# Layer-0 norm weights by a product with ones, squares and fold out of PSUM, new load costs in the planner

## The chip, the cores and the metric

The kernel runs on one core of a Trainium2 chip. The metric is the device time of one execution in microseconds; the median of several executions is compared. The engines are TensorE (PE, with its weight loads shown apart as PEld), VectorE (DVE), ScalarE (ACT), GpSimd (POOL) and SyncE (SP), which issues all the DMA transfers here.

## The reference

A two-layer encoder trunk takes one step for 512 prompt tokens and 64 sample tokens (576 rows of 1024 channels). Each layer norms x, makes one wide projection, runs three mixers (differential attention, sparse attention with a learned index, retention), gates and merges them, and adds an output projection to x. Keys, values and states are outputs too. Cut to its frame:

```python
for l in range(DEPTH):                       # 2 layers; 1024 cached keys for the sample rows
    z = rmsnorm(x, norm_g[l]) @ w_in[l]      # 1024 x 8132, split into the operands of A, B, C and the gates
    oa = diff_attention(...)                 # A: 4 heads, two softmax maps each, T5 bias
    ob = dsa_attention(...)                  # B: lightning index, top-k keys, 8 heads
    oc = rmsnorm(retention(...), c_gn_g[l])  # C: 4 heads with decay, rotary, running state
    br = stack([oa * silu(ag), ob * silu(bg), oc * silu(cg)])
    proj = einsum('btnw,nwd->btnd', br, w_branch[l])
    x = x + sum(sigmoid(mg) * proj) @ w_out[l]

def rmsnorm(x, g):
    return x * rsqrt(mean(x * x, -1) + EPS) * g
```

## The kernel before

**Tiles.** The 576 rows stand in five tiles of rows, four of 128 and one of 64 (the sample). Every large product is made of three: operands are split into a rounded part (hi) and the rest (lo), and PE adds hi x hi, hi x lo and lo x hi in one PSUM accumulation. `wload` (line 535) fetches a weight block of 512 rows x 256 columns by DMA into `wraw`, casts it on ACT to `whi` (line 549) and subtracts on DVE, or on POOL where the step is marked with `*`, to `wlo` (line 550). `wload_idx` (line 555) does the same for the index weights with casts in line 566. `proj_tok` (line 659) and `proj_ch` (line 682) are the loops of matmuls over such blocks.

**Stages.** Per layer `x_norm(t)` (line 590) squares a tile of x on ACT with a running sum (line 601, in layer 0 alone), takes the power -0.5 of the mean on POOL (line 507), scales the tile by that and by the norm weights on DVE (line 611), and transposes it on PE by products with the identity into a PSUM tile named `s` (line 616), from where ACT casts it to `xh` (line 618) and DVE subtracts it to `xl`. The norm weights `gx` are two tiles `P` of 128 x 512, which a DMA with a partition step of 0 fills (line 587). Line 804 is the index projection, the first large product of a layer, line 1018 the transposes of queries and keys of mixer A, line 1070 its logits. At the end of the layer `out_proj(u)` (line 1369) runs for either half of 512 columns: for each row tile it loads the residual into `xr` (a tile named `sg`), makes 24 matmuls into a PSUM tile `pj` (line 1402; for the sample tile 16 matmuls whose lower half ACT copies to `up`, a tile `P`, in line 1396, and which DVE adds back), scales and adds on DVE (line 1405) and, in layer 0, squares the result on ACT into a PSUM tile `s` for the running sum of the next layer's norm (line 1411; only the sum is used).

**Buffers.** Tiles of one name take turns in a fixed number of buffers: two `sg`, four `P`, four `r`, two `wraw`, three `whi`, two `wlo`; in PSUM three `pj`, two `s`, three `t`. A new tile waits until the last use of the one that had its buffer.

**Order.** The program is traced once in the order of `STEPS` (lines 90 to 128), one string per layer. A step is a name, a number and a `*` or not, and up to four biases. Then `Order.plan()` (line 279) puts all instructions into an order by a list scheduler: each has a cost by `_cost`, waits cost `LAG` and `SLOT`, and whenever an engine is free the ready instruction goes first whose traced position plus bias is least. The biases belong to PE, to the other engines, to SP, and to a spread over the step. `pin()` fixes the order of each engine. So an engine works strictly in this order, and an instruction that is not ready holds up all behind it. DMAs are in SP's order; the scheduler has a cost for each, from its bytes and the length of its contiguous runs.

## Time and profile before

| | |
|---|---|
| time of three runs | median 1425.64 us, from 1422.21 to 1428.57 |
| time of the profiled execution | 1423.9 us |
| span of the profiled execution | 1422.1 us |
| mean granted PE clock | 0.993 |
| PE busy | 1370.1 us, 96% of the span |
| DVE busy | 1030.6 us, 72% |
| ACT busy | 718.5 us, 51% |
| POOL busy | 383.0 us, 27% |
| DMA | 129.60 MB, 32% of 16 DMA engines |

The span runs from the first to the last instruction of the profiled execution; its time has 1.8 us more round it. Shares of an engine are shares of the span, and PE's own busy time counts its matmuls, whether at full clock or at half. An engine's idle time is put down to what released it: the last semaphore before the instruction that ended the wait. A granted clock of 1.00 is the full one, 2.4 GHz, and 0.50 the lower level, 1.2 GHz.

### The profile page before, as it was taken

What the parts mean: (1) busy time and instruction counts of PE and PEld (TensorE: products, weight loads), DVE (VectorE), ACT (ScalarE), POOL (GpSimd) and SP (SyncE); (2) the same over time, 40 slices, a digit from 0 to 9 for tenths busy, and PEclk for the clock granted to TensorE, in tenths of its full rate; (3) what the DMA queues carried; (4) which work ended last, traced back from release to release, by engine and by line L of the source; (5) the groups of instructions that cost most, each with busy time, mean ns of one, the idle gap of its engine ahead of it and who ended that gap; (6) DMA issues with size and microseconds to landing.
All of it is one profiled execution on the core that took longest, in us unless ns stands there. A gap on an engine that the chain in (4) does not pass through costs nothing.

```text
span 1422.1 us, 26631 instructions
## 1 busy us (share of the span) xinstructions
PE 1370.1 (96%) x9974; PEld 1296.9 (91%) x9974; DVE 1030.6 (72%) x2517; ACT 718.5 (51%) x1733; POOL 383.0 (27%) x356
## 2 busy tenths in 40 slices
PE   6999999999999999999989999999999999999998
PEld 5999999999989999998789999999989999899976
DVE  6689799997766787553378567999987777765442
ACT  5543455566656666432253344655546667565320
POOL 1633353344332300100130473412421333010000
PEclk9999999999999999999989999999999999999999
DMA  8533332343422312234432221434322312222343
GB/s 201 145 94 87 100 101 85 79 108 94 102 66 63 90 51 79 74 104 130 132 116 66 68 78 49 128 92 110 99 75 67 80 46 73 60 67 60 90 137 100
DMA packets 179994, 129.60 MB, mean 91 GB/s; under 512 B 65452, under 2 KB 168920, under 8 KB 179864
## 3 DMA queue, kind: packets, MB, share of 16 engines
q1 hardware_dynamic: 179864, 127.90, 32.2%
q8 instruction: 78, 1.28, 0.4%
q14 instruction: 52, 0.43, 0.1%
HBM read 114.84 MB, written 13.03 MB: 90 GB/s over the span
## 4 chain that ended last, share of the span: by engine, by line
PE 55%; DVE 9%; DMA 4%; ACT 4%; issue 2%; POOL 1%; DVEq 0%; ACTq 0%; POOLq 0%; SPq 0%
PE pj L690 28%; PE pj L678 7%; PE pj L1402 5%; DMA wraw<-in_w_in_dram 2%; DMA wraw<-in_w_out_dram 2%; PE s L1253 1%; DVE wlo L550 1%; PE t L1266 1%; DVE u L885 1%; POOL wlo L550 1%; DVE m L884 1%; ACT whi L549 1%; PE s L1070 1%; DVE s L520 1%; PE t L1085 1%
## 5 line engine op out<-in xcount | busy, mean ns | idle before, releaser
L550 POOL TENSOR_TENSOR wlo<-wraw,whi 128x1024 fp32r<-128x1024 f32 x62 | 151.2, 2452 | 311.4 <-PE pj L690 183.7
L549 ACT CAST whi<-wraw 128x1024 fp32r<-128x1024 f32 x148 | 155.2, 1049 | 138.6 <-DMA wraw<-in_w_in_dram 79.5
L690 PE MATMUL pj<-xh,whi 128*128 128x288 f32 x1216 | 206.0, 300 | 4.7 <-ACT whi L549 2.2
L690 PE MATMUL pj<-xh,wlo 128*128 128x288 f32 x1216 | 202.3, 298 | 0.2 <-DVE wlo L550 0.2
L690 PE MATMUL pj<-xl,whi 128*128 128x288 f32 x1216 | 202.1, 297 | 0.0
L690 PEld LDWEIGHTS pj<-xh,whi 128*128 128x128 f32 x1216 | 174.0, 188 | 8.7 <-ACT whi L549 3.3
L690 PEld LDWEIGHTS pj<-xl,whi 128*128 128x128 f32 x1216 | 174.9, 188 | 1.1
L690 PEld LDWEIGHTS pj<-xh,wlo 128*128 128x128 f32 x1216 | 174.2, 188 | 1.9 <-DVE wlo L550 0.6
L550 DVE TENSOR_TENSOR wlo<-wraw,whi 128x1024 fp32r<-128x1024 f32 x86 | 110.0, 1291 | 60.0 <-PE pj L690 49.1
L690 PE MATMUL pj<-u,whi 128*128 128x288 f32 x768 | 124.8, 297 | 0.1
L678 PE MATMUL pj<-whi,xh 128*128 128x256 f32 x768 | 116.1, 283 | 2.6 <-DVE ssn L701 1.7
L507 POOL TENSOR_TENSOR ssn<-ssn,mh 128x4 f32<-128x4 f32 (+1 forms) x70 | 67.8, 972 | 179.5 <-DVE ssn L506 160.1
L678 PE MATMUL pj<-wlo,xh 128*128 128x256 f32 x768 | 115.8, 283 | 0.0
L884 DVE MAX8 m<-u 128x8 f32<-128x1088 f32 (+2 forms) x128 | 113.5, 888 | 1.5
L678 PE MATMUL pj<-whi,xl 128*128 128x256 f32 x768 | 113.1, 281 | 0.0
L885 DVE MATCH_REPLACE8 u<-m,u 128x1088 f32<-128x1088 f32 (+2 forms) x128 | 112.0, 875 | 0.1
L690 PEld LDWEIGHTS pj<-u,whi 128*128 128x128 f32 x768 | 109.4, 189 | 1.7 <-DVE sg L1348 0.6
L678 PEld LDWEIGHTS pj<-whi,xh 128*128 128x128 f32 x768 | 100.3, 188 | 5.2 <-DVE ssn L701 2.7
L678 PEld LDWEIGHTS pj<-wlo,xh 128*128 128x128 f32 x768 | 100.0, 188 | 1.5 <-issue 0.3
L678 PEld LDWEIGHTS pj<-whi,xl 128*128 128x128 f32 x768 | 98.6, 188 | 0.8 <-issue 0.5
L728 POOL TENSOR_TENSOR u<-r,u 128x512 fp32r<-128x512 f32 x24 | 31.9, 1339 | 172.5 <-ACT u L727 172.4
L1339 ACT ACTIVATE sg<-pj 128x288 f32<-128x288 f32 x96 | 38.9, 410 | 61.4 <-PE pj L690 60.9
(299 smaller groups left out, 2694.9 us busy)
## 6 DMA issues: line engine op xcount, KB each, us to landing
wraw<-in_w_in_dram SPq DMA_DIRECT2D x116, 512.0 KB, 3.8
wraw<-in_w_branch_dram SPq DMA_DIRECT2D x24, 512.0 KB, 3.8
wraw<-in_w_out_dram SPq DMA_DIRECT2D x16, 512.0 KB, 4.2
wraw<-in_w_in_dram SPq DMA_DIRECT2D x20, 256.0 KB, 3.4
r<-in_cache_a_k_dram SPq DMA_DIRECT2D x64, 64.0 KB, 2.5
r<-in_cache_a_v_dram SPq DMA_DIRECT2D x16, 256.0 KB, 2.9
D<-grep SPq DMA_DIRECT2D x24, 112.0 KB, 2.2
out_dram<-u SPq DMA_DIRECT2D x18, 128.0 KB, 2.0
```

The source lines that it names most:

```text
L507: ptt(ss, ss, mh[:ss.shape[0], :1].to_broadcast(list(ss.shape)), op=OP.pow)
L520: nc.vector.tensor_tensor_reduce(s, s, d, 1.0, init, OP.add, OP.min, out)
L549: nc.scalar.copy(hi[:, :n], raw[:, :n])
L550: (ptt if beside[0] else tt)(lo[:, :n], raw[:, :n], hi.bitcast(F32)[:, :n], op=OP.subtract)
L678: mm(ps[:M, :ncol], a[:, k, q], b[:, k, :ncol], start=(i == 0 and k == 0), stop=(i == 2 and k == 7))
L690: mm(ps[:, :288], a[:, k, c], b[:, k, q], start=(i == 0 and k == 0), stop=(i == 2 and k == kt - 1))
L728: ptt(lo, k, hi.bitcast(F32), op=OP.subtract)
L884: nc.vector.max(m8[:sc.shape[0]], sc)
L885: nc.vector.match_replace(sc, m8[:sc.shape[0]], sc, SENT)
L1070: mm(s[:, :w], Q[c][:, hh, tq], K[c + 2 * i][:, hh, :w], start=i == 0, stop=i == 1)
L1339: lambda q, ps: act(sg[:, q], ps, AF.Tanh, scale=0.5))
L1402: mm(ps[:M], src[:, c0:c0 + M], (hv, hv, lv)[i][k], start=(i == 0 and k == 0), stop=(i == 2 and k == 7))
```

## The change

Four things are changed.

1. In layer 0 each half of the norm weights is loaded as one row of 512 into a tile `sg`, a product with a row of 128 ones spreads it over the partitions into a PSUM tile `t`, and ACT copies that into `gx`. Layer 1 loads them as before.
2. In `out_proj` the squares go into `xr`, the residual tile, which is not needed by then, instead of a PSUM tile `s`. The copy `up` of the fold goes into a tile `sg` instead of `P`.
3. The planner has another cost for loads: 17 more per run of 256 to 512 elements, and three times as much where the source's partition step is 0. At most eight DMAs are under way in its account: one starts no earlier than the end of the eighth before it.
4. `STEPS` has other biases, another order of the steps in each layer, and other marks `*` (74 weight subtractions on POOL instead of 66).

The diff, with one line of `STEPS` of before and of after for each layer:

```diff
-x0+700,5000,-300,-17600 x1+3700,-800,-2600 x2+-4200,-2200,-8100,400 w0+0,1300,7800,1900 x3+-400,6700,200
...
+x0+-6800,-1600,2000 x3+13800,-2800,-10000,-700 pv0+800,5200,24900,-5000 x1+-3900,-2100,-700,-3700
...
-kc0+-300,-14000,2400,1600 pw0*+1000,4500,-300,2600 x0+-39500,-13300,-100,-300 x1+-25500,9700,-5600,4200
...
+x0+3000,7100,-2900,-31400 x1+0,-7600,500,-300 pw0*+6600,-10200,-2700,-800 x2+100,-26300,-500,2000
...
@@ -210,7 +209,8 @@
         if e == "SP":
             n = cols(outs[0]) * outs[0].ap[0][1]
             run = min(self._run(o) for o in ins[:1] + outs[:1])
-            return n / run * max(36.0, run / 6.0) / 16
+            each = max(36.0, run / 6.0 + 17.0 * (256 <= run <= 512))
+            return n / run * each / 16 * (3 if ins[0].ap[0][0] == 0 else 1)
         if e == "PE":
             n = cols(outs[0])
             fast = "float32r" in str(ins[0].dtype)
@@ -356,6 +356,8 @@
                     k = min(other)[1]
             cost, shared = ops[k][4], ops[k][6]
             order[e].append(k)
+            if e == "SP" and len(order[e]) > 8:
+                t = max(t, end[order[e][-9]])
             start[k] = t
             if e == "SP":
                 clock[e] = t + 500
@@ -462,6 +464,8 @@
     id2 = cs[:, C_ID2:C_ID2 + 64]
     mh = sb(8, "mh")
     nc.vector.memset(mh, -0.5)
+    one = sb(128, "zk")
+    nc.vector.memset(one[:1], 1.0)
     PS = [sb(256, "Ps") for _ in range(2)]
     for p in PS:
         nc.gpsimd.memset(p[:, 192:], 0.0)
@@ -584,7 +588,14 @@
         xhv, xlv = v3(xh, 8), v3(xl, 8)
         gx = [sb(512, "P") for _ in range(2)]
         for i in range(2):
-            dma(gx[i], bcast_row(norm_g[l, 512 * i:512 * i + 512], 512))
+            g = norm_g[l, 512 * i:512 * i + 512]
+            if l:
+                dma(gx[i], bcast_row(g, 512))
+            else:
+                row, gp = sb(NTOK, "sg"), pb("t")
+                dma(row[:1, :512], g.rearrange("(o c) -> o c", o=1))
+                mm(gp, one[:1], row[:1, :512], start=True, stop=True)
+                nc.scalar.copy(gx[i], gp)
         ready = {}
 
         def x_norm(t):
@@ -1392,9 +1403,9 @@
                     for k in range(8):
                         mm(ps[:64], msv[k // 4][:, k % 4, 0:64], lv[k], start=False, stop=k == 7,
                            skip_group_check=True)
-                    up = sb(512, "P")
-                    nc.scalar.copy(up[:64], ps[64:128])
-                    tt(ps[:64], ps[:64], up[:64], op=OP.add)
+                    up = sb(NTOK, "sg")[:64, :512]
+                    nc.scalar.copy(up, ps[64:128])
+                    tt(ps[:64], ps[:64], up, op=OP.add)
                 for i in range(3 if t < 4 else 0):
                     for k in range(8):
                         src = (mhi, mlo, mhi)[i][k // 2]
@@ -1407,8 +1418,7 @@
                     d = o_yp[0, 128 * t:128 * t + 128, :] if t < 4 else o_ys[0]
                 else:
                     d = yscr[128 * t:128 * t + M, :]
-                    jk = pb("s")
-                    act(jk[:M], y, AF.Square, accum_out=PSQ_[t][:M, u:u + 1])
+                    act(xr[:M], y, AF.Square, accum_out=PSQ_[t][:M, u:u + 1])
                 dma(d[:, c], y)
 
 
```

**What moves, at three places.** The rows are "line, operation, result <- operands, shape, count". The start, on PE: `s` are the transposes of x, `t_177` is the product for the bias windows, `pj` the index projection. Before:

```order
L616 MATMUL s_107<-cs_70,u_63 128x128
L616 MATMUL s_115<-cs_70,u_63 128x128 x4
L616 MATMUL s_107<-cs_70,u_63 128x128 x3
L479 MATMUL t_177<-P_172,rb_175 12x352
L616 MATMUL s_132<-cs_70,u_64 128x128 x4
L616 MATMUL s_140<-cs_70,u_64 128x128 x4
L804 MATMUL pj_277<-whi_210,xh_84 128x392 x2
L804 MATMUL pj_321<-whi_210,xh_84 128x392 x2
```

After (the lines of the changed kernel are shifted: 616 is 627, 804 is 815; `zk_74` is the row of ones, `sg_90` and `sg_95` the norm weights):

```order
L597 MATMUL t_91<-sg_90,zk_74 128x512
L597 MATMUL t_96<-sg_95,zk_74 128x512
L627 MATMUL s_117<-cs_70,u_63 128x128 x4
L627 MATMUL s_125<-cs_70,u_63 128x128 x4
L627 MATMUL s_142<-cs_70,u_66 128x128 x3
L627 MATMUL s_150<-cs_70,u_66 128x128 x4
L627 MATMUL s_142<-cs_70,u_66 128x128
L815 MATMUL pj_284<-whi_214,xh_86 128x392 x2
L815 MATMUL pj_284<-wlo_217,xh_86 128x392 x2
```

Two products with ones stand at the head, the product for the bias windows has gone behind, and the tile after the first is the one of `u_66`. On ACT, before, up to the casts of the first two index weight blocks (`r` are the squares, `xh` the casts of the transposes):

```order
L601 ACTIVATE r_99,ss_98<-u_63 128x512
L1093 CAST qd_3341<-cs_70 64x2x64 x2
L601 ACTIVATE r_124,ss_123<-u_64 128x512
L601 ACTIVATE r_126,ss_123<-u_64 128x512
L601 ACTIVATE r_149,ss_148<-u_65 128x512
L601 ACTIVATE r_151,ss_148<-u_65 128x512
L618 CAST xh_84<-s_107 128x4x128
L618 CAST xh_84<-s_115 128x4x128
L601 ACTIVATE r_184,ss_183<-u_66 128x512
L601 ACTIVATE r_186,ss_183<-u_66 128x512
L566 CAST whi_210<-wraw_207 128x2x196
L566 CAST wlo_213<-wraw_207 128x2x196
```

And after:

```order
L612 ACTIVATE r_109,ss_108<-u_63 128x512
L1104 CAST qd_3118<-cs_70 64x2x64 x2
L598 COPY P_88<-t_91 128x512
L612 ACTIVATE r_134,ss_133<-u_66 128x512
L612 ACTIVATE r_136,ss_133<-u_66 128x512
L598 COPY P_89<-t_96 128x512
L612 ACTIVATE r_178,ss_177<-u_64 128x512
L612 ACTIVATE r_180,ss_177<-u_64 128x512
L629 CAST xh_86<-s_117 128x4x128
L629 CAST xh_86<-s_125 128x4x128
L570 CAST whi_214<-wraw_211 128x2x196
L570 CAST wlo_217<-wraw_211 128x2x196
```

Two copies into `P` have come in, and the casts of the index weights stand behind five squares instead of seven.

The layer boundary, on PE: `pj_8683` and `pj_8748` are tiles of the output projection's last half (layer 0), `s` the transposes of layer 1's first x tile, `pj_9001` its index projection. Before:

```order
L1402 MATMUL pj_8683<-wlo_8660,u_8269 128x512 x2
L1402 MATMUL pj_8683<-wlo_8666,u_8075 128x512 x2
L1402 MATMUL pj_8683<-u_8672,u_7881 128x512 x2
L1402 MATMUL pj_8683<-u_8678,u_8463 128x512 x2
L616 MATMUL s_8887<-cs_70,u_8473 128x128 x4
L616 MATMUL s_8895<-cs_70,u_8473 128x128 x4
L804 MATMUL pj_9001<-whi_8868,xh_8831 128x392 x2
L804 MATMUL pj_9001<-wlo_8871,xh_8831 128x392 x2
L804 MATMUL pj_9001<-whi_8877,xh_8831 128x392 x2
```

After (line 1402 is 1413):

```order
L1413 MATMUL pj_8718<-wlo_8671,u_7891 128x512 x2
L1413 MATMUL pj_8718<-u_8677,u_8279 128x512 x2
L627 MATMUL s_8849<-cs_70,u_8483 128x128 x4
L1413 MATMUL pj_8718<-u_8683,u_8473 128x512 x2
L1413 MATMUL pj_8748<-u_8682,u_8473 128x512
L627 MATMUL s_8857<-cs_70,u_8483 128x128 x4
L1413 MATMUL pj_8748<-u_8682,u_8473 128x512
L1413 MATMUL pj_8748<-whi_8664,u_8086 128x512 x2
L1413 MATMUL pj_8748<-whi_8670,u_7892 128x512 x2
L1413 MATMUL pj_8748<-u_8676,u_8280 128x512 x2
L1413 MATMUL pj_8748<-u_8682,u_8474 128x512 x2
L1413 MATMUL pj_8748<-wlo_8665,u_8085 128x512 x2
```

The transposes of the first tile stood behind the last product of the projection; now they stand in the middle of two of its tiles. On ACT at the same place, before (line 1411 is the square, 566 the cast of index weights, 618 the cast of the transposes):

```order
L566 CAST wlo_8871<-wraw_8865 128x2x196
L566 CAST wlo_8880<-wraw_8874 128x2x196
L1411 ACTIVATE s_8709,ss_8478<-u_8473 128x512
L1411 ACTIVATE s_8740,ss_8479<-u_8474 128x512
L1411 ACTIVATE s_8771,ss_8480<-u_8475 128x512
L1411 ACTIVATE s_8802,ss_8481<-u_8476 128x512
L549 CAST whi_9217<-wraw_9216 128x1024
L1411 ACTIVATE s_8828,ss_8482<-u_8477 64x512
L618 CAST xh_8831<-s_8887 128x4x128
L618 CAST xh_8831<-s_8895 128x4x128
```

After (1421, 570 and 629):

```order
L1391 CAST u_8676<-wraw_8674 128x1024
L1391 CAST u_8682<-wraw_8680 128x1024
L570 CAST whi_8886<-wraw_8883 128x2x196
L1421 ACTIVATE sg_8686,ss_8488<-u_8483 128x512
L629 CAST xh_8831<-s_8849 128x4x128
L629 CAST xh_8831<-s_8857 128x4x128
L1421 ACTIVATE sg_8716,ss_8489<-u_8484 128x512
L1421 ACTIVATE sg_8746,ss_8490<-u_8485 128x512
L629 CAST xh_8831<-s_8876 128x4x128
L629 CAST xh_8831<-s_8868 128x4x128
```

The squares alternate with the casts of the transposes, and they write `sg`; a cast of index weights stands ahead of the first tile's square.

The middle of layer 1, on PE, where the logits of mixer A begin (`t` are transposes of queries and keys, `s_13552` the first logits). Before:

```order
L1018 MATMUL t_12761<-cs_70,z_12751 128x128 x2
L1018 MATMUL t_12802<-cs_70,z_12792 128x128
L1018 MATMUL t_13233<-cs_70,z_13224 128x128 x2
L1018 MATMUL t_12802<-cs_70,z_12792 128x128
L1070 MATMUL s_13552<-u_12571,u_13184 128x256
L1070 MATMUL s_13552<-u_12573,u_13184 128x256
L1070 MATMUL s_13558<-u_12572,u_13185 128x256
```

After (1018 is 1029, 1070 is 1081, 678 is 689; `s_13399` is the first logits):

```order
L689 MATMUL pj_13169<-whi_13035,xh_8831 128x256 x4
L689 MATMUL pj_13169<-whi_13041,xh_8831 128x256 x2
L1029 MATMUL t_13080<-cs_70,z_13071 128x128 x2
L689 MATMUL pj_13169<-whi_13041,xh_8831 128x256 x2
L689 MATMUL pj_13169<-whi_13035,xl_8832 128x256 x4
L689 MATMUL pj_13169<-whi_13041,xl_8832 128x256 x4
L689 MATMUL pj_13169<-wlo_13036,xh_8831 128x256 x4
L689 MATMUL pj_13169<-wlo_13042,xh_8831 128x256 x4
L1081 MATMUL s_13399<-u_12418,u_13031 128x256
L1081 MATMUL s_13399<-u_12420,u_13031 128x256
```

Between the last transposes and the first logits 18 products of the projection have come. On ACT in the middle of layer 0, before (`aTs` is the copy of a transposed attention tile, `P_5028` the one before it):

```order
L980 ACTIVATE P_5006,z_5015<-s_4994,nm_5013 128x512
L980 ACTIVATE P_5007,z_5015<-s_4995,nm_5013 128x384
L980 ACTIVATE Ps_75,z_5015<-t_4996,nm_5013 128x192
L513 COPY P_5028<-t_5023 128x512
L549 CAST whi_5617<-wraw_5616 128x1024
L513 COPY aTs_5037<-t_5038 128x128
L950 ACTIVATE P_5054<-o_4855 128x512
```

After (513 is 517, 980 is 991; `aTs_5332` is the same copy):

```order
L991 ACTIVATE P_5301,z_5310<-s_5289,nm_5308 128x512
L991 ACTIVATE Ps_77,z_5310<-t_5291,nm_5308 128x192
L991 ACTIVATE P_5302,z_5310<-s_5290,nm_5308 128x384
L517 COPY P_5323<-t_5318 128x512
L517 COPY aTs_5332<-t_5333 128x128
L961 ACTIVATE P_5349<-o_5150 128x512
```

The cast of a weight block between the two copies has gone from there.

## Rows read from the trace of the kernel before

**Rows 1.** The page, part 1: busy us, share of the span, instructions.

```profile
PE 1370.1 (96%) x9974; PEld 1296.9 (91%) x9974; DVE 1030.6 (72%) x2517; ACT 718.5 (51%) x1733; POOL 383.0 (27%) x356
```

**Rows 2.** Windows by stage: length, busy PE, PEld, DVE, ACT, POOL, PE clock, DMA, GB/s.

```profile
0.00:50.00 50.00, 36.95 (x229) 33.38 (x230) 33.79 (x108) 28.43 (x82) 14.26 (x26) 1.00 0.72 177
50.00:650.00 600.00, 591.98 (x4520) 572.14 (x4520) 462.46 (x1139) 322.20 (x775) 190.99 (x164) 1.00 0.32 88
650.00:750.00 100.00, 90.42 (x465) 75.96 (x465) 50.19 (x120) 38.26 (x95) 16.14 (x25) 0.93 0.44 129
750.00:1350.00 600.00, 586.57 (x4472) 564.56 (x4471) 460.14 (x1120) 317.85 (x767) 161.60 (x142) 1.00 0.28 77
1350.00:1423.00 73.00, 64.21 (x297) 50.83 (x295) 23.99 (x33) 11.79 (x16) 0.00 (x0) 0.96 0.35 116
```

**Rows 3.** Timeline of the start: start, us, engine, line, tiles, count [idle before, releaser].

```profile
2.11 0.91 SPq L587 DMA_DIRECT2D P<-in_norm_g_dram  x2
...
8.66 1.42 DVE L611 SCALAR_TENSOR_TENSOR u<-u,ss,P 128x512 f32<-128x512 f32 x2 [3.25 <-DMA P<-in_norm_g_dram]
...
10.12 1.97 PE L616 MATMUL s<-cs,u 128*128 128x128 f32 x8 [10.12 <-DVE u L611]
...
13.24 1.33 PE L479 MATMUL t<-P,rb 32*12 32x352 f32 x2 [1.15 <-DMA rb<-in_rel_bias_dram]
...
16.84 1.67 PE L804 MATMUL pj<-whi,xh 128*128 128x392 f32 x4 [0.37 <-DVE whi L567]
...
26.61 0.63 ACT L601 ACTIVATE r<-u 64x512 f32<-64x512 f32 x1 [1.79 <-DMA u<-in_x_sample_dram]
```

**Rows 4.** Timeline of PE at the layer boundary.

```profile
709.54 1.09 PE L1402 MATMUL pj<-wlo,u 128*128 128x512 f32 x4
710.47 1.09 PE L1402 MATMUL pj<-u,u 128*128 128x512 f32 x4
715.04 1.08 PE L616 MATMUL s<-cs,u 128*128 128x128 f32 x4 [3.49 <-DVE ss L607]
717.97 1.11 PE L616 MATMUL s<-cs,u 128*128 128x128 f32 x4 [1.85 <-ACT s L1411]
```

**Rows 5.** Timeline of DVE and POOL in that gap.

```profile
711.59 0.69 DVE L1405 SCALAR_TENSOR_TENSOR u<-pj,sg 128x512 f32<-128x512 f32 x1 [2.33 <-PE pj L1402]
...
713.56 0.56 POOL L507 TENSOR_TENSOR ss<-ss,mh 128x1 f32<-128x1 f32 x1 [0.77 <-DVE ss L506]
```

**Rows 6.** Windows in and behind that gap (columns as rows 2).

```profile
711.00:716.00 5.00, 1.51 (x7) 0.83 (x5) 3.41 (x12) 2.75 (x9) 3.08 (x5) 0.78 0.73 184
...
718.00:725.00 7.00, 7.00 (x32) 6.86 (x33) 6.18 (x12) 2.50 (x5) 0.99 (x1) 0.57 0.38 141
```

**Rows 7.** The page, part 6: DMA issues, KB each, median us from issue to landing.

```profile
sg<-in_x_prompt_dram SPq DMA_DIRECT2D x8, 256.0 KB, 3.0
...
P<-in_norm_g_dram SPq DMA_DIRECT2D x4, 256.0 KB, 4.5
...
gcol<-in_a_subln_g_dram SPq DMA_DIRECT2D x2, 0.5 KB, 3.0
```

**Rows 8.** Groups of ACT by line and shape: count | busy, mean ns | idle before, releaser.

```profile
L618 ACT CAST xh<-s 128x512 fp32r<-128x512 f32 x16 | 9.2, 587 | 9.4 <-PE s L616 9.3
...
L1411 ACT ACTIVATE s<-u 128x512 f32<-128x512 f32 x8 | 4.7, 592 | 11.6 <-DVE u L1405 11.6
...
L601 ACT ACTIVATE r<-u 128x512 f32<-128x512 f32 x7 | 4.4, 627 | 6.4 <-DMA u<-in_x_prompt_dram 6.4
...
L601 ACT ACTIVATION_READ_ACCUMULATOR r<-u 128x1 f32 x7 | 1.3, 191 | 0.0
```

**Rows 9.** Timeline of ACT and PE in the two middles.

```profile
405.27 1.04 ACT L549 CAST whi<-wraw 128x1024 fp32r<-128x1024 f32 x1 [2.48 <-DMA wraw<-in_w_in_dram]
...
406.54 0.49 PE L1119 MATMUL t<-vs,aTs 128*128 128x128 f32 x2 [1.50 <-ACT aTs L513]
...
1059.54 1.02 PE L1070 MATMUL s<-u,u 128*128 128x256 f32 x4 [1.78 <-DVE u L1028]
```

More of the change, by code (lines that the diff above doesn't have):

```diff
@@ new lines @@
+cq0*+3700,4500,-200 gc0*+-7000,0,-11500,3300 cv1*+9200,4800,3000,800 ca0+2700,-3600,11400,-11200
+wg0+-6000,1900,4400,2900 kc0+0,500,0,-4400 wg3+-13900,-7000,300,-3500 cq1*+4200,4100,-400 sc0+0,-4400,2700,7800
+wg1+4200,700,-900,-200 gc1+15200,-1400,500,3000 ca1+-8300,8800,9700,1700 top1+-3300,26200,4200,-3200
+sc1+-2300,19200,0,-6000 i2+-8800,6700,4900 ak0*+3000,-3800,400,6900 ga0+-800,-10300,-200,6500
+av0*+-6300,4200,-400,600 mc2*+58900,-800,-500,400 aa1+-7300,15100,3400,3200 mc3*+2000,-3100,-7100,100
@@ new lines @@
+mc2*+1200,400,-1700,900 av1+5900,-1700,1700,11000 aa1+35900,2000,3000 mc3+46200,1500,-400,-100
+ak1+59500,1000,400,1800 mc1+-5900,-800,0,11100 mc0*+-21300,1900,-1100,3300 sa0+9400,0,1000,-700
+vc0+-100,2400,4200,4900 aq1*+0,1700,4600 ga1+0,3100,2000,3000 aa3+-12600,0,-3600,7100 gb0*+0,-400,6100,1000
+aa2+-2300,-3600,-2400,2400 top2+1700,2300,-5400,2600 bq0+32200,6800,600,-14600 top4+87700,-4600,1100,-800
+sa1+4800,500,4700,-600 ma1+55700,3100,-1600,4000 kc1+-1000,300,700,-1500 top1+-2400,-3300,6600
@@ L127 @@
+w0+-2700,-18500,3200,-1300 gb1*+-43900,2400,3700,17100 bp0+-48500,100,0,1200 bq1+-600,6100,-6000,12100
+bp1+-64300,-12400,0,400 bs0+0,0,-400,1200 bs1+1800,3300,-4700 sb0+10300,2500,-1600,-7600 ma0+7700,1800,200,22900
+wg1+0,-10200,1700,-2100 ma2*+300,0,1600,-11400 ma3+2500,8800,-3100,1800 sb1+-300,2600,-4600
+mb1+6600,800,-400,-2700 mb2+0,5800,800 mb3*+-600,1000,2700,2300 mb0+-3200,-2900,-100,500
+wg3+-1800,-500,10600,-3200 wg0+0,6300,-600 y0+-200,-3100,13600,5400 y1+5000,-3800,100
 """)
```

50 lines of the change are left out of this document (17 added, 33 removed).

## The prediction

> **What bounds the kernel now.** I read the views in this order. First the busy times: TensorE's array (PE) works 1370.1 us, 96% of the span [rows 1]. So the kernel is a queue of matmuls, and what can be won is the time in which PE stands still, 52.0 us in all, or runs at its lower clock. Next the same by stage [rows 2]: PE stands still 13.1 us in the first 50 us, 8.0 in the 600 us of the first layer's middle, 9.6 in the 100 us round the layer boundary, 13.4 in the second layer's middle and, up to the end of the span, 7.9 in the last output projection. The clock column says 1.00 everywhere but at the boundary (0.93) and at the end (0.96). No other engine is near full over a stage: VectorE (DVE) is busy 462 of 600 us in either middle. So I went on to the three timelines: start, boundary, and the longer single waits of the middles.
>
> At the start PE waits until 10.12 us for DVE's scaling of the first x tile; that had waited 3.25 us more for the norm weights, two loads that write one row to 128 partitions, issued at 2.11 and there at 8.66 [rows 3]. The steady stream begins with the first index product at 16.84. At the boundary PE's last product of layer 0 ends at 711.56 and the first transposes of layer 1 start at 715.04, the second four at 717.97 (waits of 3.49 and 1.85 us) [rows 4]. The reader should see the chain between: scaling and residual add at 711.59, then the square, the power at 713.56, then PE at 715.04 [rows 4, 5]; no work of layer 1 was queued into the output projection. After the gap the clock is down: 0.78 in 711 to 716, 0.57 in 718 to 725, although PE is then busy without a pause [rows 6].
>
> **The change, part by part.** All sums are against the profiled execution, 1423.9 us with a span of 1422.1; it lies 1.7 under the median of the three runs shown (1425.64, from 1422.21 to 1428.57), so half of that, 0.9, is added to the result.
>
> *Norm weights of layer 0 by a product with ones.* Two loads of 256 KB go, two of 2 KB come at the same places in SP's queue; two products, two ScalarE (ACT) copies are added. A 0.5 KB load takes 3.0 us to land, the old ones 4.5 as a median [rows 7]; 2.11 + 3.0 = 5.1. The nearest product in kind is L479, two instructions of 352 columns in 1.33 us [rows 3]; for 512 columns 1.33 x 512/352 = 1.93 us. So the first product ends at 7.0, its copy (0.59, as the cast of an equal tile out of PSUM [rows 8]) at 7.8, the scaling of 0.7 at 8.7, PE's first transposes at about 9.0 instead of 10.12. The second product ends at 9.0; both lie where PE stood still. ACT is now the busiest there. In its order stand one square and a small cast, done before 7.2; the first copy, to 7.8; two squares, each 0.63 and 0.19 for the read-out of its sum [rows 8] (1.6); the second copy (0.6); two squares (1.6); two casts of x at 0.59 (1.2); one cast of index weights, 392 columns (0.45 by 0.59 x 392/512). That makes 13.2. DVE's subtraction, taken like its 0.69 at 711.59 [rows 5], and the hand-over add 0.8, so the index products start at 14.0 to 14.2 instead of 16.84: 2.6 earlier. The sample's x tile moves up from 24th to 14th in SP's order; ACT had waited for it 1.79 us, to 26.61 [rows 3], and PE had stood still 1.3 us there, which I count as half saved. Together 3.2, taken as **-3.0 us**. Lower bound: only the 1.0 us of the first transposes comes through. Upper: 2.6 + 1.3 and 1.1 from the traffic that no longer shares the engines, 5.0.
>
> The page "DMA: Bandwidth & Descriptors" of the Trainium skill (Rules for kernel authors) speaks against small loads: under 64 KB a transfer pays mostly overhead, so 2 KB would land hardly sooner than a large one. The trace agrees in part: 3.0 us for 0.5 KB against 4.5 for 256 KB [rows 7]. Were the rule taken whole, landing would be 2.11 + 4.5 = 6.6 and this term -1.5.
>
> *Squares out of PSUM.* Ten squares now write the residual tile they no longer need. A square into PSUM took 592 ns, the same from and to SBUF 627 [rows 8]: 0.35 us in ten, on an ACT that is idle most of that stage, so nothing. Each residual tile is held one square longer, 0.8 us, before the next load into its buffer, which takes 3.0 [rows 7]. PE spends 24 matmuls at 0.93/4 = 0.23 us on a tile [rows 4], 5.6 us, and two tiles are in hand; the load is hidden. Were it not, it would be 0.8 a tile, 8 in ten.
>
> *What that frees.* The squares took turns with the transposes for the two "s" buffers; the fold took "P" buffers that the next layer's norm weights need. Both gone, the planner puts the transposes of tiles 0 and 1 of layer 1 into the output projection, as the PE order shows. Gone are 3.49 + 1.85 of waiting. At the lower clock PE spent 7.0 us at 0.57, (1 - 0.57) x 7.0 = 3.0, and some 0.6 just before [rows 6]: 8.9 in all. New: PE holds the matmuls behind a transpose that is not ready. The chain from the end of tile 0's last product to the transposes took 3.48 us before [rows 4]; the new order leaves 16 matmuls between, 3.7 us, so tile 0 just fits. Tile 4 is last and has a fold in its chain; there I allow 2.0 us. Term: **-7.0 us**. Bounds: -8.9 with no new wait, -3.0 if tiles 0 and 4 both wait as long as before and only the clock's share is saved.
>
> *Fold into an "sg" buffer.* 4 copies of 0.6 us as before. In the last projection the next residual load then waits for the fold, but its 3.0 us end within the 5.6 of the tile under way, and the last tile's chain has no fold. Nothing; 1 us at most.
>
> *Planner.* Costs of loads and the limit of eight change every engine's order and 8 weight subtractions go from DVE to GpSimd (POOL), busy 27% of the span [rows 1]. The work is the same, and the attention rows stand within some 10 us of work of their old places. I looked at the two longest middle waits with a plain cause. At 405.27 ACT had taken up a weight cast whose load was 2.48 us late, and a copy behind it made PE wait 1.50 [rows 9]; in the new ACT order no cast stands ahead of that copy. At 1059.54 PE waited 1.78 for DVE's key parts [rows 9]; between the transposes and the logits stood almost nothing, now 18 products of 256 columns. Together 3.3, taken as **-3.0 us** for both middles. The other 18 us of waiting there are dozens of waits mostly under 1 us, which a new order deals out anew: bounds -7 and +4, a third of them gone or as much again as is saved.
>
> Sum: -3.0 - 7.0 - 3.0 = -13.0; 1423.9 - 13.0 + 0.9 = 1411.8, **1412 us**.
>
> **The rivals.** (a) *The boundary stays shut*: the change does not do what it says. ACT works in order, and the cast of index weights (L570) now stands ahead of tile 0's square; if its load is late, square, scaling and transposes are late, and PE holds three tiles of matmuls behind them. For it: rows 9 show just such a cast. Against it: that load is issued some 6 us before. It gives back the 7.0: 1419.
> (b) *The middles get longer* where the old order fitted the chip by chance: +6 instead of -3, 1421. For it: every row moves. Against: no stage of the middle loses over 2.3% of its time now, and the skeleton is kept.
> (c) *Slower*: casts block ACT in the middles. Each cast of weights that ACT reaches before its load is there costs PE 1.5 us as at 406.54 [rows 9]. For a time over 1433 it takes 21 us more, 14 such casts over both layers. If the planner's new load costs were too low for most loads this could be; before, only a few did it. 1433 to 1438.
> (d) *Better*: no new waits at the boundary, 5.0 at the start, 7 in the middles: 1404.
>
> **How the numbers follow.** Forecast 0.62 (its own range 1406 to 1418), (a) 0.13, (b) 0.11, (c) 0.08, (d) 0.06. The ends of all bounds together are 1404 (13.0 + 1.9 + 2.0 + 4.0 more won would be 20.9 off 1424.8) and, with the smallest terms (-1.0 and -3.0) and the middles at +4, 1425; (b) in full adds 2. I give 1404 to 1426, which leaves out (c) and the ends of (b) and (d). A measurement of this kernel can tell about 0.5% from no change: faster is under 1418.5, slower over 1432.8. The forecast, (d) and a third of (a), with its 1419 just at the bound, are faster, 0.72; the rest of (a) and (b) the same, 0.20; (c) slower, 0.08.
>
> **What would show it.** First products by about 5 us and index products by 14 at the start; at the boundary a clock of 1.00 through the first transposes and no PE wait over 2 us between the last projection tiles; about 18 us of PE waits in both middles; span near 1410. Wrong would be: a PE wait on an L627 transposes group of over 3 us with ACT behind a load (a); middles with over 25 us of waits (b, c); or index products not before 16 us.

## The result and the profile after

The changed kernel takes 1407.59 us (median of four runs, 1406.32 to 1411.14), the kernel before 1425.02 (1422.21 to 1428.57). The ratio is 0.988 with an interval of 0.9852 to 0.9909: 17.4 us, 1.2% faster, where 13 were forecast. The span of the profiled execution went from 1422.1 to 1405.5 us.

First the same windows by stage as [rows 2] of before, of the changed kernel (length, busy PE, PEld, DVE, ACT, POOL, PE clock, DMA, GB/s):

```profile
0.00:50.00 50.00, 43.21 (x267) 38.09 (x268) 36.79 (x120) 30.80 (x89) 8.59 (x24) 1.00 0.63 160
50.00:650.00 600.00, 594.02 (x4515) 576.78 (x4514) 464.00 (x1134) 322.63 (x775) 204.23 (x167) 1.00 0.33 91
650.00:750.00 100.00, 94.44 (x553) 82.08 (x552) 54.93 (x130) 40.64 (x104) 21.09 (x27) 1.00 0.44 128
750.00:1350.00 600.00, 587.25 (x4442) 566.46 (x4441) 465.88 (x1111) 318.36 (x764) 172.58 (x147) 1.00 0.28 78
1350.00:1406.00 56.00, 49.26 (x210) 37.85 (x208) 14.32 (x17) 5.87 (x7) 0.00 (x0) 0.98 0.35 118
```

Length less PE's busy time is its idle time: 6.8, 6.0, 5.6, 12.8 and 6.2 us (up to the span's end at 1405.5), 37.3 in all. Before it was 13.1, 8.0, 9.6, 13.4 and 7.9, 52.0 in all. So 14.7 of the 16.6 us of the span are idle time. The totals can be compared; the last two windows only with care, since at one and the same time the changed kernel is up to 16.6 us further in its work. PE's busy time fell by 1.9 only, although it holds 3.75 us of new products; the clock at the boundary, 0.93 before, is 1.00.

The start, from the timeline of the changed kernel:

```profile
2.12 0.61 SPq L596 DMA_DIRECT2D sg<-in_norm_g_dram  x2
...
4.54 3.75 PE L597 MATMUL t<-sg,zk 1*128 1x512 f32 x4 [4.54 <-DMA sg<-in_norm_g_dram]
...
6.61 0.59 ACT L598 COPY P<-t 128x512 f32<-128x512 f32 x1 [1.53 <-PE t L597]
7.30 0.75 DVE L622 SCALAR_TENSOR_TENSOR u<-u,ss,P 128x512 f32<-128x512 f32 x1 [1.90 <-ACT P L598]
...
8.21 1.11 PE L627 MATMUL s<-cs,u 128*128 128x128 f32 x4
...
14.23 1.02 PE L815 MATMUL pj<-whi,xh 128*128 128x392 f32 x2
```

The rows are there 2.4 us after their issue, the two products take 3.75, and the copy of the first and the scaling follow at once. The transposes start at 8.21 instead of 10.12 and the index products at 14.23 instead of 16.84 [rows 3].

The row that leads to the index products is ACT's. Its first square of the second x tile, before and after:

```profile
9.84 0.63 ACT L601 ACTIVATE r<-u 128x512 f32<-128x512 f32 x1 [4.78 <-DMA u<-in_x_prompt_dram]
```

```profile
7.22 0.63 ACT L612 ACTIVATE r<-u 128x512 f32<-128x512 f32 x1
```

Before, ACT stood still 4.78 us until that tile had landed; now it does not wait, and starts 2.62 us earlier. From there to the index products it is 7.0 us in both kernels, through squares and casts. The tile is issued behind the loads of the norm weights, at 3.06 before and at 2.77 now.

The boundary, first PE's timeline, then two rows of ACT:

```profile
691.65 0.62 PE L1413 MATMUL pj<-u,u 128*128 128x512 f32 x2
692.11 0.60 PE L627 MATMUL s<-cs,u 128*128 128x128 f32 x4
692.47 0.94 PE L1413 MATMUL pj<-u,u 128*128 128x512 f32 x3
693.25 0.60 PE L627 MATMUL s<-cs,u 128*128 128x128 f32 x4
```

```profile
687.17 0.52 ACT L570 CAST whi<-wraw 128x392 fp32r<-128x392 f32 x1 [3.08 <-DMA wraw<-in_w_in_dram]
689.38 0.63 ACT L1421 ACTIVATE sg<-u 128x512 f32<-128x512 f32 x1 [1.69 <-DVE u L1416]
```

No row of PE here has an idle time in brackets: the transposes of layer 1 lie among the products of layer 0, where [rows 4] showed waits of 3.49 and 1.85. The cast of index weights that stands ahead of the first square did wait 3.08 us for its load, but it was done at 687.69, 1.7 us before that square had its operand. The same stretches as in [rows 6] now read:

```profile
711.00:716.00 5.00, 5.00 (x40) 4.68 (x38) 4.72 (x15) 2.85 (x10) 0.68 (x2) 1.00 0.80 251
718.00:725.00 7.00, 7.00 (x52) 6.79 (x52) 6.33 (x27) 4.42 (x16) 2.73 (x5) 1.00 0.24 48
```

PE is busy all the time at clock 1.00, where it was 0.78 and 0.57.

### The profile page after: what moved, and what is told of

Same layout as the page of the kernel before. It is cut to its first block, busy times and chain, and to the rows that moved or that the text cites. A ratio compares the mean times of both kernels' runs of the same rounds, so it can differ in the third digit from the quotient of the medians.

```text
span 1405.5 us, 26681 instructions
## 1 busy us (share of the span) xinstructions
PE 1368.2 (97%) x9978; PEld 1301.3 (93%) x9978; DVE 1035.9 (74%) x2510; ACT 718.3 (51%) x1735; POOL 406.5 (29%) x364
## 5 line engine op out<-in xcount | busy, mean ns | idle before, releaser
L554 POOL TENSOR_TENSOR wlo<-wraw,whi 128x1024 fp32r<-128x1024 f32 x70 | 169.6, 2437 | 376.1 <-PE pj L701 257.1
L701 PE MATMUL pj<-xh,wlo 128*128 128x288 f32 x1216 | 205.4, 299 | 0.0
L689 PE MATMUL pj<-whi,xh 128*128 128x256 f32 x768 | 119.9, 285 | 1.6 <-DVE u L930 1.3
L689 PE MATMUL pj<-whi,xl 128*128 128x256 f32 x768 | 116.2, 284 | 0.0
L689 PEld LDWEIGHTS pj<-whi,xl 128*128 128x128 f32 x768 | 101.5, 188 | 0.9 <-issue 0.5
L701 PE MATMUL pj<-u,wlo 128*128 128x288 f32 x384 | 68.6, 301 | 5.0 <-DVE wlo L554 4.7
```

The source lines that it names most:

```text
L554: (ptt if beside[0] else tt)(lo[:, :n], raw[:, :n], hi.bitcast(F32)[:, :n], op=OP.subtract)
L689: mm(ps[:M, :ncol], a[:, k, q], b[:, k, :ncol], start=(i == 0 and k == 0), stop=(i == 2 and k == 7))
L701: mm(ps[:, :288], a[:, k, c], b[:, k, q], start=(i == 0 and k == 0), stop=(i == 2 and k == kt - 1))
```

## The experiments

Twelve kernels were run, each against the kernel before on the same chip. Two ideas were open. **Parts**: start, boundary and middles each give their share by the mechanism that the prediction names. **Table**: the gain sits in the new order as a whole, and the parts in the code matter little. A difference between two kernels below is one of medians; where it is small, the intervals of the ratios to before are set beside it.

### The boundary: four runs

**Undo one half in the changed kernel: the fold in P, or the squares in PSUM.** Either shuts the gate, the way of layer 1's first transposes into the projection: the planned order then has no transposes inside the projection, where the changed kernel has 16. On PE the order moves round the boundary alone.

```diff
-                    up = sb(NTOK, "sg")[:64, :512]
-                    nc.scalar.copy(up, ps[64:128])
+                    up = sb(512, "P")
+                    nc.scalar.copy(up[:64], ps[64:128])
```

> The changed kernel with one edit undone: the fold copy of the output projection goes into a tile P again; the squares stay in the residual tile, and biases, planner and norm weights are those of the changed kernel. The planned order then has no transposes of layer 1 inside the last output projection (16 in the changed kernel). Theory (the boundary gate: fold and squares each bar the next layer's norm by themselves, so undoing one shuts it): a wait of 3 us or more before the first transposes of layer 1, clock down for some 7 us after it, 7 to 9 us slower than the changed kernel, about 1416. Rival (the boundary was gained by the squares alone, or by the new order of the steps): 1407 to 1410.

Measured: 1425.0 us, ratio to before 0.9998 (0.9977 to 1.0019). The whole gain is gone, 17.4 us, twice what was expected. The timeline tells why:

```profile
707.09 0.58 ACT L1407 COPY P<-pj 64x512 f32<-64x512 f32 x1 [0.40 <-PE pj L1404]
...
708.88 0.97 SPq L593 DMA_DIRECT2D P<-in_norm_g_dram  x2
...
712.55 6.71 DVE L622 SCALAR_TENSOR_TENSOR u<-u,ss,P 128x512 f32<-128x512 f32 x10 [0.68 <-DMA P<-in_norm_g_dram]
...
719.31 1.97 PE L627 MATMUL s<-cs,u 128*128 128x128 f32 x8 [12.26 <-DVE u L622]
```

The buffers P go in turn, so the norm weights of layer 1 are issued behind the fold of the last tile. When they come, all five tiles are ready to be scaled, and the planned order of DVE puts the half that PE needs first last of ten: 6.71 us more. PE waits 12.26, and runs at a lower clock behind it:

```profile
719.00:735.00 16.00, 14.92 (x90) 13.91 (x90) 9.15 (x26) 6.96 (x19) 0.87 (x2) 0.76 0.03 7
```

By an estimate from this row the clock costs (1 - 0.76) x 14.92 = 3.6 us, so that wait and clock make 15.8 of the 17.4.

```diff
-                    act(xr[:M], y, AF.Square, accum_out=PSQ_[t][:M, u:u + 1])
+                    jk = pb("s")
+                    act(jk[:M], y, AF.Square, accum_out=PSQ_[t][:M, u:u + 1])
```

> The changed kernel with the squares in PSUM tiles s again, the fold in sg; only the order round the boundary moves, no transposes stand inside the projection. The run with the fold in P lost 17 us, because its norm weights were issued only after the fold (at 708.9) and all ten scalings stood ahead of the first transposes. Here the norm weights' buffers are free. Theory (the gate itself is worth 7 to 10 us, the rest there was the late norm weights): 1415 to 1418. Rival (a shut gate always costs this table 15 or more): 1422 to 1426.

Measured: 1415.7 us, ratio 0.9931 (0.9909 to 0.9954) against the changed kernel's 0.988 (0.9852 to 0.9909): 8.1 us slower by medians and 7.3 by the ratios, as expected. Here the norm weights are early, and what is left at the boundary is the gate alone: a PE wait for a square, and a lower clock behind it.

```profile
711.93 0.66 PE L627 MATMUL s<-cs,u 128*128 128x128 f32 x4 [3.27 <-ACT s L1422]
```

```profile
711.00:716.00 5.00, 3.98 (x18) 3.06 (x19) 3.49 (x8) 2.81 (x6) 0.54 (x1) 0.77 0.86 246
716.00:718.00 2.00, 2.00 (x14) 2.00 (x14) 0.69 (x1) 1.44 (x3) 0.00 (x0) 0.72 0.45 131
```

In the 100 us round the boundary PE is idle 8.9 us in this trace and 5.6 in the changed kernel's, and these two rows give an estimated 1.5 us of clock: 4.8 of the 8.1 are seen there. Another 2.1 us in the trace lie far off, in one DVE instruction of layer 0's middle that took 2.78 us instead of 0.72 (shown below, under the middles). So the 8.1 may be somewhat more than the gate's own price.

**Do it alone in the kernel before: the buffers, then the buffers and one number.** The first has the two diffs above the other way round, and nothing else.

> The kernel before with the squares in the residual tile and the fold in sg, and nothing else; the planned order still has no transposes inside the output projection, because the old biases do not ask for them. Theory (freeing the buffers is needed but not enough; the table must put the norm there): no change, 1424 to 1426. Rival (taking the squares out of PSUM saves by itself, since transposes no longer wait for them, 1.85 us and the clock): 1419 to 1422.

Measured: 1426.1 us, ratio 0.9997 (0.9978 to 1.0015): nothing. With both buffers free the planned order stays shut. The transposes take the two `s` buffers in traced order, so tile 0's come first; and by the old table tile 0's products in the projection end last, since a spread of -6300 puts a step's late instructions ahead.

```diff
-y1+21000,-3400,-400,-6300
+y1+21000,-3400,-400
```

> The kernel before with the squares in the residual tile, the fold in sg, and one number of the table taken out: the spread of -6300 of the last output projection of layer 0, which let its first tile end last. Now the planned order has 24 transposes of layer 1 inside that projection; on PE only the 150 or so instructions round the boundary stand elsewhere, all else is the order of the kernel before. Theory (the gate needs both, free buffers and the first tile ending first, and its gain stays): the waits of 3.5 and 1.9 us and the half clock go, 7 to 10 us faster than before, 1415 to 1418. Rival (the gain is given back in layer 1, whose order waits for loads and cache work instead): 1421 to 1425.

Measured: 1417.9 us, ratio 0.9956 (0.9939 to 0.9974), 6.3 us faster than before with the old start and costs and, but for that number, the old table; a little under the 7 to 10 expected. The two windows of [rows 6] here:

```profile
711.00:716.00 5.00, 5.00 (x26) 3.65 (x24) 3.24 (x6) 2.37 (x6) 2.62 (x4) 1.00 0.18 60
718.00:725.00 7.00, 7.00 (x51) 6.51 (x50) 6.09 (x19) 4.20 (x15) 1.41 (x3) 1.00 0.78 232
```

So the gate needs three things, two free buffers and the first tile ending first. It is worth 6 to 8 us by itself, and layer 1 doesn't give it back: the rival of this run, 1421 to 1425, has fallen.

### The start: three runs

**Undo the product with ones in the changed kernel.**

```diff
-                row, gp = sb(NTOK, "sg"), pb("t")
-                dma(row[:1, :512], g.rearrange("(o c) -> o c", o=1))
-                mm(gp, one[:1], row[:1, :512], start=True, stop=True)
-                nc.scalar.copy(gx[i], gp)
+            dma(gx[i], bcast_row(norm_g[l, 512 * i:512 * i + 512], 512))
```

> The changed kernel with the norm weights of layer 0 loaded as before, written to 128 partitions by a load with partition step 0, no product with ones; all else as in the changed kernel. Theory (the landing of those two loads sets the start): the first transposes at 10 us again instead of 8.2, index products at 16 to 17 instead of 14.2, 2.5 to 4.5 us slower, 1410 to 1412. Rival (ACT's row of squares and casts sets the start, and the new order of x tiles and loads carries the gain): index products by 15, 1408 to 1409.

Measured: 1409.7 us, ratio 0.9883 (0.9847 to 0.9919). That is 2.1 us by medians; by the ratios it can't be told from the changed kernel. The spans of the traces are 1407.9 and 1405.5, but here too 2.1 us lie in the one DVE instruction of layer 0's middle, so they don't settle it. PE's and ACT's rows show what happens at the start:

```profile
7.01 1.11 PE L618 MATMUL s<-cs,u 128*128 128x128 f32 x4 [7.01 <-DVE u L613]
10.08 1.12 PE L618 MATMUL s<-cs,u 128*128 128x128 f32 x4 [1.96 <-DVE u L613]
...
16.75 1.02 PE L806 MATMUL pj<-whi,xh 128*128 128x392 f32 x2
```

```profile
10.82 0.63 ACT L603 ACTIVATE r<-u 128x512 f32<-128x512 f32 x1 [2.08 <-DMA u<-in_x_prompt_dram]
```

One half of the weights came early, and the first transposes start at 7.01, even earlier than in the changed kernel; "10 us again" was a miss. Yet the index products are 2.5 us later than 14.23, within the 16 to 17 expected. So the landing of the norm weights is not what they wait for. The second x tile, which is issued behind those two loads, lands late: ACT's square of it starts at 10.82. In all six traces with the two loads of 256 KB that square starts between 9.84 and 10.82, in all eight with the 2 KB rows between 7.07 and 8.63. So by these traces the product with ones wins its time through the traffic that it takes away ahead of that tile; no run moved that tile's load alone.

**The product with ones alone, in the kernel before.**

> The kernel before with the product with ones for the norm weights of layer 0 and nothing else. Theory (the landing of the two loads held the start): first transposes by 8.5 us instead of 10.1, index products 1 to 2 us earlier than 16.84, since the old order of x tiles stays and ACT has more in its row; 1423 to 1425. Rival (as in the changed kernel, 2.6 us and more come through): 1421 to 1422.

Measured: 1436.3 us, ratio 1.0094 (1.0063 to 1.0124), 11.8 us *slower*. The start itself went as the theory said (first transposes at 8.35, index products at 15.49); both times that were expected fell. The loss comes later. SP's, ACT's and PE's rows, and a window:

```profile
29.30 0.57 SPq L604 DMA_DIRECT2D u<-in_x_sample_dram  x1
```

```profile
35.19 0.63 ACT L610 ACTIVATE r<-u 64x512 f32<-64x512 f32 x1 [3.15 <-DMA u<-in_x_sample_dram]
```

```profile
38.55 1.37 PE L625 MATMUL s<-cs,u 64*128 64x64 f32 x8 [4.93 <-DVE u L620]
```

```profile
30.00:50.00 20.00, 12.38 (x62) 11.13 (x63) 10.38 (x32) 6.62 (x25) 7.23 (x8) 0.66 0.52 139
```

With its old table the planner moved the sample's x tile behind output transfers, to 29.30. PE then stood still, 7.6 us in this window where it was 0.1 before, and ran at a granted clock of 0.66; by an estimate that costs (1 - 0.66) x 12.38 = 4.2 us, and both together are as much as the whole loss. The same edit is worth +12 us with one table and, by medians, -2 with another.

**The rows of norm weights ahead of everything, with no other instruction moved.**

```diff
+        sp = order["SP"]
+        sp[:] = sp[3:5] + sp[:3] + sp[5:]
```

> The changed kernel with the two rows of norm weights at the head of SP's order, ahead of the first x tile and the identity; no other instruction of any engine moves. Theory (the landing of the rows and the products with ones, at half clock, hold the first scaling): products at about 3.2 instead of 4.5 us, first transposes 0.5 to 1 us earlier, index products 0 to 0.5 earlier since ACT's row of squares stands ahead of them; 1406.5 to 1407.6, not to be told from the changed kernel. Rival (the x tile, now 0.6 us later, is what holds the start): first transposes 0 to 0.6 us later, 1407.6 to 1408.5.

Measured: 1412.5 us (1406.5 to 1415.7), ratio 0.9883 (0.9839 to 0.9927); by the ratio the same as the changed kernel. At the start neither idea was right:

```profile
2.16 3.75 PE L599 MATMUL t<-sg,zk 1*128 1x512 f32 x4 [2.16 <-DMA sg<-in_norm_g_dram]
8.16 1.12 PE L629 MATMUL s<-cs,u 128*128 128x128 f32 x4 [2.25 <-DVE P L480]
...
15.64 1.02 PE L817 MATMUL pj<-whi,xh 128*128 128x392 f32 x2
```

```profile
6.66 0.58 ACT L600 COPY P<-t 128x512 f32<-128x512 f32 x1
...
8.63 0.63 ACT L614 ACTIVATE r<-u 128x512 f32<-128x512 f32 x1 [1.39 <-DMA u<-in_x_prompt_dram]
```

The products came 2.4 us earlier and won nothing. The copy of their result stands behind a small cast of the constants on ACT, whose load now came later, and starts at 6.66 instead of 6.61; the first transposes are where they were. The index products are 1.4 us later than in the changed kernel, since ACT's square of the second x tile is: it waits for that tile until 8.63 instead of starting at 7.22. The span is 7.8 us longer than the changed kernel's; these 1.4 are all of it that the start shows. The "half clock" of the expectation is not in the clock column, which shows 1.00; what that column is worth at the start stands at the end of this document.

### The middles: the table and the planner's costs, five runs

**The table alone, and the changed kernel without the new costs.** The first is the kernel before with the string `STEPS` of the changed one; the second has the diff below, its boundary is open and its start new.

> The kernel before with the changed kernel's table of steps and biases alone: its norm loads, its squares in PSUM, its fold in P, its planner costs. Theory (the parts in the code carry start and boundary, the table only the middles): 3 to 5 us faster than before, 1420 to 1422, with the boundary shut as before. Rival (the table carries nearly all): 1410 to 1413.

> The changed kernel with the planner's old load costs and no limit of eight; the code of start and boundary and the table as changed, the boundary open in the planned order. Theory (the table is fitted to the orders that the new costs give; under the old costs its biases put casts and loads wrongly): 20 to 50 us slower than the changed kernel, 1428 to 1458, with new waits in both middles. Rival (the 60 us of the run with the table alone came from its shut boundary and its start; the costs hardly matter): 1406 to 1412.

```diff
-            each = max(36.0, run / 6.0 + 17.0 * (256 <= run <= 512))
-            return n / run * each / 16 * (3 if ins[0].ap[0][0] == 0 else 1)
+            return n / run * max(36.0, run / 6.0) / 16
...
-            if e == "SP" and len(order[e]) > 8:
-                t = max(t, end[order[e][-9]])
```

Measured: 1486.0 us (ratio 1.042, 1.0387 to 1.0453) and 1470.1 (1.032, 1.0293 to 1.0347). The table that goes with the new costs loses 62 us without them, more than the 20 to 50 expected, and both ideas of the table alone, which had it faster than before, fell. The limit of eight has no part in that: without it the planned orders of PE, ACT, DVE and POOL are the same instruction by instruction, and of 513 DMAs three pairs of neighbours change places. Where the time goes shows in three windows of the changed kernel with the old costs:

```profile
50.00:650.00 600.00, 585.10 (x4418) 564.74 (x4416) 454.72 (x1119) 318.23 (x765) 205.08 (x167) 0.99 0.32 88
750.00:1350.00 600.00, 565.67 (x4200) 542.27 (x4199) 457.95 (x1096) 307.87 (x754) 172.90 (x152) 0.97 0.26 72
1300.00:1340.00 40.00, 27.60 (x147) 23.19 (x147) 21.75 (x63) 24.48 (x58) 0.00 (x0) 0.79 0.11 30
```

The middles idle 14.9 and 34.3 us instead of 6.0 and 12.8. In all PE is idle 73.3 us instead of 37.3, and busy 1395.4 instead of 1368.2: 36 us of the loss are waits; the 27 of busy time go with a mean granted clock of 0.981 for 0.998. In the last window PE has attention work left and few products to put between it; a group of PE in that window (count | busy, mean ns | idle before, releasers), and then the same group in the changed kernel over its whole span:

```profile
L1312 PE MATMUL t<-cs,P 128*128 128x128 f32 x28 | 7.8, 400 | 7.7 <-ACT Ps L988 4.0 <-ACT P L1300 3.8
```

```profile
L1315 PE MATMUL t<-cs,P 128*128 128x128 f32 x56 | 9.3, 277 | 0.3 <-DVE r L521 0.3
```

These transposes wait 7.7 us in the one window and 0.3 us in all in the changed kernel, where the attention is over by 1300 us.

**Are the new costs better, or only the ones that the table was made with?** The kernel before with the new costs (the diff above the other way round), and the changed kernel with another number in them, 8 or 25 for 17.

> The kernel before with the planner's new load costs and the limit of eight, its old table and old code. Theory A (costs nearer to what loads take make better orders of themselves; ACT's waits for late weight loads, 79.5 us before and 29.1 in the changed kernel, fall): 1400 to 1424. Theory B (a table is fitted to the costs it was found with, and any other costs spoil the order): 20 to 60 us slower than before, 1445 to 1485, whatever ACT's waits for loads do.

> The changed kernel with 8 instead of 17 in the planner's cost of a run of 256 to 512 elements, all else as changed: half of the way back to the old cost of such runs. Theory A (the right cost is what counts): between the changed kernel and the run with the old costs, 1415 to 1445. Theory B (any cost but the one of the table spoils it): about as slow as with the old costs, 1440 to 1480.

> The changed kernel with 25 instead of 17 in that cost, loads counted as even longer. Theory A (loads counted longer are asked for earlier, so ACT waits no more for them than in the changed kernel; a small loss): 1405 to 1420, ACT's waits for weight loads under 35 us. Theory B (the table is spoilt on either side): 1430 to 1480.

```diff
-            each = max(36.0, run / 6.0 + 17.0 * (256 <= run <= 512))
+            each = max(36.0, run / 6.0 + 25.0 * (256 <= run <= 512))
```

Measured: 1482.8 us for the kernel before with the new costs (ratio 1.0379, 1.0342 to 1.0416), 1462.7 with 8 in place of 17 (1.0238, 1.0196 to 1.0279), 1463.3 with 25 (1.0239, 1.0197 to 1.0282). Theory B holds on all three: on either side of the table's own number, and with the old table under the new costs, the loss is 55 to 56 us. ACT's waits for late weight loads, 79.5 us before and 29.1 in the changed kernel, are no guide to it. From the list of waits (us in total, times, longest), the old table under the new costs, and then 25:

```profile
ACT whi L552 <- DMA wraw<-in_w_in_dram: 35.4, 20, 7.0
```

```profile
ACT whi L553 <- DMA wraw<-in_w_in_dram: 16.8, 15, 5.3
```

Both wait far less for loads than before, and both are slower than it, by 3.8 and 2.4%. The higher the cost, the less ACT waits for loads (46.3 us with 8, 29.1 with 17, 16.8 with 25); that does not make the kernel faster unless the biases are fitted to it. For the largest group of loads the new cost is also the nearest to the trace before:

```profile
wraw<-in_w_in_dram SPq DMA_DIRECT2D x116, 512.0 KB, 3.8
```

By the planner's code such a load, with nothing ahead of it, is there after 3.8 us with 17, 3.2 with the old cost, 3.5 with 8 and 4.0 with 25 (an estimate, since the measured median holds waits in the queue too). Which of the thousands of moved instructions makes each stall was not isolated.

## Why the prediction was right, and where not

**The sum.** Forecast -13.0, measured -17.4; the sign and the range held, the likeliest time was 4 us high. The mechanism at the boundary was right, the one at the start in part. The step that went wrong is how the planner was counted. Undoing start and boundary one at a time accounts for 2.1 and 8.1 of the 17.4; the rest comes with the table and its costs, which no run could take back without losing far more, so where the missing 4 us come from stays open.

**Start, -3.0.** In PE's idle time of the first 50 us 6.3 us went, of which 3.75 are new products: 2.5 net, with the index products 2.6 earlier. Two products were put at 3.86 by the scaled row and took 3.75; the first transposes were forecast for about 9.0 and came at 8.21, since the rows landed in 2.4 us and not in 3.0. ACT's wait for the sample's tile (1.79 in [rows 3]) is gone. The index products, forecast for 14.0 to 14.2, came at 14.23, but that is partly luck, for two steps of the row were off and cancel. DVE's subtraction of those weights:

```profile
13.62 0.56 DVE L571 TENSOR_TENSOR whi<-wraw,whi 128x392 fp32r<-128x392 f32 x1
```

ACT was done with the cast of index weights (11.50, 0.52 us) at 12.02, not at 13.2, and DVE, busy with scalings and subtractions of x until then, began the subtraction only at 13.62. And the row silently takes the second x tile to be there when ACT comes to it. Before, it was not, by 4.78 us; the prediction read the wait for the norm weights and not this one, and had the traffic that goes away in its upper bound alone. By the experiments it is this wait that the product with ones takes away: undone in the changed kernel, the index products fall back by 2.5 of the 2.6 us; alone, with the old order of ACT's squares, it brings 1.35.

The prediction weighed a rule of the Trainium skill ("DMA: Bandwidth & Descriptors", Rules for kernel authors): under 64 KB a transfer pays mostly overhead. What the prediction drew from it, that 2 KB would land hardly sooner than 256 KB, 4.5 us after the issue, did not come: the trace says 2.4 here and 1.4 where the rows are issued first. The measurement decides against that inference; the rule itself speaks of what such a transfer pays for and not of when it lands.

**Boundary, -7.0.** Undone alone it costs 8.1, done alone it gives 6.3. In the trace 4.0 us of idle time went in the 100 us round it, and the 3.6 us of clock that the prediction counted, 7.6 together. The clock was also lower earlier in the projection, 0.94 before in 670 to 700 against 1.00 now, but that can't be put down to the boundary: the kernel with the buffers alone, boundary shut, shows 1.00 there too.

The 2.0 us that were allowed for new waits behind unready transposes did not come; that term was too cautious. "Tile 0 just fits" held: no wait at 692.11.

**"Both gone, the planner puts the transposes into the projection."** Wrong as a cause, right as a fact. Freeing the buffers alone did nothing; a spread in the table had to go too. And the fold's buffer was priced at "1 us at most" for the copy only: left in P it costs 17 us in the new table, because of the norm weights queued behind it. The cost of an edit that only frees something lies in who is queued for it.

**Squares and fold in SBUF, nothing.** Held: a square takes 630 ns instead of 592 [rows 8], and no residual load is late by it.

**Middles, -3.0.** In the windows as they stand, idle time went from 21.4 to 18.7, -2.7. To compare the same work, the second middle has to end as far from the end of the span, 55.5 us, in both. The rows are before, up to 1366.6 and behind it, and then the end of the changed kernel:

```profile
750.00:1366.60 616.60, 601.36 (x4564) 577.53 (x4563) 470.54 (x1137) 324.29 (x777) 161.60 (x142) 1.00 0.28 79
1366.60:1422.10 55.50, 49.42 (x205) 37.86 (x203) 13.58 (x17) 5.35 (x6) 0.00 (x0) 0.95 0.33 109
```

```profile
1350.00:1405.50 55.50, 49.26 (x210) 37.85 (x208) 14.32 (x17) 5.87 (x7) 0.00 (x0) 0.99 0.36 119
```

So cut, the second middle's idle time went from 15.2 to 12.8 us, -2.5. The four runs that leave the changed table and its costs alone (fold in P, squares in PSUM, norm weights as before, rows first) have 12.7 to 13.2 there, the two of the boundary with the old table 14.8 and 15.0: this gain is the new order's. In the first middle it went from 8.0 to 6.0, but the same four runs have 7.9 to 8.2. Their difference from the changed kernel is one instruction; in its trace and in that of the squares in PSUM:

```profile
261.77 0.72 DVE L1088 SCALAR_TENSOR_TENSOR P<-P,Z,P 128x512 f32<-128x512 f32 x1
```

```profile
261.98 2.78 DVE L1088 SCALAR_TENSOR_TENSOR P<-P,Z,P 128x512 f32<-128x512 f32 x1
```

In all four it took 2.6 to 2.9 us, and PE waited 2.3 behind it. Why it was short in the changed kernel's profiled execution is open; the 2 us of the first middle are luck of that execution and no gain of the order. The wait of 1.50 behind the cast at 405 and the one of 1.78 for DVE's key parts [rows 9] are gone from the list of PE's waits, as read from the order, and so is a longer one that the prediction had left out (2.02 at 1025, behind a weight cast); others of up to 2.0 came, such as

```profile
559.78 1.06 PE L701 MATMUL pj<-u,wlo 128*128 128x288 f32 x6 [1.96 <-DVE wlo L554]
```

So the size, about -2.5 without that luck, was near for the pair of table and costs. As a statement on the planner it was wrong: "the work is the same" hid that either alone is worth +55 to +60 us. Rival (b) was priced at +6 and rival (c) at over 21; a table that doesn't fit its costs would have been far beyond both. The mechanism of (c), casts that block ACT, is not what those runs show either: 16.8 us of such waits went with 1463 us.

**Last projection.** Over the last 55.5 us of the span PE is idle 6.1 us before and 6.2 after: the idle time is the same, and the prediction had no term for it. The 7.9 and 6.2 of the windows by stage are of stretches of 72.1 and 55.5 us. The clock there, 0.95 before and 0.99 after, is anywhere from 0.94 to 1.00 in the six runs just named, so it tells nothing of the change.

## What to carry to other kernels

A wait between two stages can have several bars at once: count the buffers, the queue behind each, and which tile the earlier stage finishes first, since removing all but one of them can bring nothing. Where a planner with hand-fitted biases sets the order, its costs and its biases are one thing: a cost that is nearer to the truth can lose 4% until the biases are fitted again, and a small edit elsewhere (here a product with ones) can lose nearly 1% by moving a load that has nothing to do with it. Read the order that comes out, at the loads as well as at the matmuls, before pricing an edit in such a kernel. At the start of a kernel, ask of every engine's first rows which load they wait for: a load that is made small can gain by what is queued behind it more than by its own landing.

## What the runs showed of the hardware

Two loads of 2 KB, one row each, were there 1.4 us after the first was issued when nothing was ahead of them (0.73 to 2.16), and 2.4 us behind the first x tile and the constants (2.12 to 4.54). The 256 KB that a step of 0 spread over 128 partitions took 4.5 as a median before [rows 7]. The 512 KB x tile issued behind them was in use at 9.84 before, 6.8 us after its issue, and at 7.22 in the changed kernel, 4.5 us after it.

A pair of products of 352 columns took 1.33 us at 13.24 in the kernel before [rows 3] and 0.76 at 19.52 in the changed one, with a granted clock of 1.00 shown in both stretches:

```profile
19.52 0.76 PE L483 MATMUL t<-P,rb 32*12 32x352 f32 x2
```

Four transposes of x took 1.04 us at 17.60 in the changed kernel and 0.60 at 18.68. So in the first 18 us or so the clock column doesn't account for PE's pace, and durations from there are no measure for the same instruction later.
